# Two attentions with V as the stationary operand, in halves of TensorE's array; one group's z gemm computed during the second attention

## The chip, the cores and the metric

One core of one Trainium2 chip runs the whole program. The metric is device time in microseconds, from launch to end. TensorE (PE in the rows) multiplies, VectorE (DVE), ScalarE (ACT) and GpSimd (POOL) do the elementwise work, and SyncE (SP) issues most of the DMA transfers. In a matmul one operand is loaded into the array first (the stationary one) and the other is streamed through it (the moving one).

## The reference, cut to what matters

Two transformer-like blocks on 512 tokens of width 1024, everything in fp32. The first has a sliding-window attention and a memory attention (4 heads of 64 each), the second a top-k sparse attention with 16 heads on 4 key/value heads, a state-space branch (SSD) in 4 groups, and a mixture of experts. The parts that the change touches:

```python
# block 1, both attentions
p = softmax(logits)                                  # [head, query, key]
out = einsum('bhsm,bmhd->bshd', p, v)
# block 2
o = jnp.einsum('bqhgk,bqkhd->bqhgd', softmax(logits), v_sel)
...
y_ssd = ssd_chunked(xh, dt, A, B, C) + d_skip * xh
y_ssd = gated_group_rmsnorm(y_ssd, z, ssd_norm)      # silu(z) gates it; z = h @ W_z, in 4 groups of 512 columns
merged = sigmoid(gate_a) * (y_attn @ w_attn_branch) + sigmoid(gate_b) * (y_ssd @ w_ssd_branch)
```

## The kernel before

Tokens are worked on in 4 tiles of 128 (`NT = 4`, `P = 128`, `T = 512`). Almost all gemms are `gemm_t`: the weight is split into a rounded part `hi` (on ACT, line 173) and a rest `lo` (on DVE or POOL, line 175), and each product is three matmuls of 128 x 512 (lines 224 to 226). One unit of `gate` is 24 of these, and one 256-column unit pair of `w2` is 48.

The order is set by generators. `mix(main, filler)` runs a chain of dependent steps and after each pulls so much of a filler gemm as the step's number says; a scheduler then fixes the order on each engine. The engines run their queues in order.

The first block's attention (`pipeline` of `logits, expo, ptrans, pvmul, otrans` over 8 units, one per 128 queries and kind) has the gemms of u and z as filler. The second block's (32 units: key/value head `kv`, pair `c` of heads, query tile `b`) has the gate gemms as filler: `gates` is a chain of 16 units, the first 5 of which run ahead of it. In both, `pvmul` multiplies the transposed probabilities (`pT`, stationary, 128 x 128) by V (moving, 64 columns) (lines 755 and 1085), DVE scales the rows by the reciprocal `r` of the softmax sum while it takes the result out of PSUM, and `otrans` transposes the scaled tile on PE (lines 768 and 1098). In the second block the transposes of four query tiles fill one PSUM tile (`pacc`, of which there is one), which ACT copies out once per head pair.

After that `block2b` runs the SSD groups. `ssd_gemm(g)` gives five gemms of 48 matmuls for group g: b and c, xs in two halves, z in two halves. Those of b, c and xs end in `conv_silu` on DVE and ACT (lines 1184 to 1196), those of z in `silu_from` (lines 450 to 455). The gemms of group 0 run first; then `ssd_chain(0)` (chunks of 128 tokens: lines 1249 to 1302) runs with the gemms of group 1 as filler, and so on. The chain's product at line 1282 has its output in partitions 0 to 63 for one head and 64 to 127 for the next.

Of the kernel before, what the change touches and what calls it, by code (L numbers as in the profile page):

```python
# [19 lines left out]
P = 128  # L20
T = 512
# [22 lines left out]
class Ker:  # L44
# [412 lines left out]

    def pipeline(self, units, stages, need):
# [65 lines left out]
    def block1(self):  # L524
# [218 lines left out]
        def pvmul(u):  # L743
            kind, n = u
            wk, r, pT = st[u][1], *st[u][4:6]
            po = self.paux()
            nj = wk // P
            for h in range(4):
                for j in range(nj):
                    if kind == 0:  # L750
                        kt = n + 1 - nj + j
                        v = sv[:, kt * P + (h // 2) * 64:kt * P + (h // 2) * 64 + 64]
                    else:
                        v = mv[:, j * 256 + h * 64:j * 256 + h * 64 + 64]
                    nc.tensor.matmul(po[:, h * 64:h * 64 + 64], pT[j][:, h * P:(h + 1) * P], v,
                                     start=(j == 0), stop=(j == nj - 1))
            o = self.ms([P, 256], "ot")
            nc.vector.tensor_tensor(o.rearrange("p (h d) -> p h d", h=4),
                                    po[:, :256].rearrange("p (h d) -> p h d", h=4),
                                    r.unsqueeze(2).to_broadcast([P, 4, 64]), op=ALU.mult)  # L760
            st[u] = o

        def otrans(u):
            kind, n = u
            o = st.pop(u)
            po = self.paux()
            for c in range(2):
                nc.tensor.transpose(po[:, c * P:(c + 1) * P], o[:, c * P:(c + 1) * P], self.ident)
            nc.vector.tensor_copy(c2(oc if kind else ob)[:, :, n * P:(n + 1) * P],
                                  po[:, :256].rearrange("p (c t) -> p c t", c=2))  # L770
# [21 lines left out]
        mix(self.pipeline(units, (logits, expo, ptrans, pvmul, otrans), 4.5), f2)  # L792
# [77 lines left out]
    def block2(self, hh, hl, ssq):  # L870
# [181 lines left out]
        def expo(u):  # L1052
# [6 lines left out]
            r = self.sm([P, 2], "xr")  # L1059
            nc.vector.reciprocal(r, s)  # L1060
            st[u].append(r)
# [17 lines left out]
        def pvmul(u):  # L1079
            kv, c, b = u  # L1080
# [1187 lines left out]
```

## Time and profile before

| | us |
|---|---|
| median of three runs | 1304.72 |
| lowest, highest | 1301.74, 1309.18 |
| the profiled execution's own time | 1306.37 |
| its span, first to last instruction | 1304.7 |
| PE, DVE, ACT, POOL busy in the span | 1245.5, 882.0, 509.1, 429.5 |
| mean granted TensorE clock | 0.98 |

An engine counts as busy from the start of an instruction to its end. Matmuls overlap (the next starts before the one before has ended), so for PE the distance from start to start is what one costs, and PE may have room though it counts as busy. An fp32 matmul that isn't split stands in the trace as two records.

### The profile page before, as it was taken

How to read it: one execution, taken by the hardware profiler on the slowest of the kernel's cores; microseconds unless marked ns; L12 is line 12 of the kernel's file. 1: busy time of each engine (PE TensorE's matmuls, PEld its weight loads, DVE VectorE, ACT ScalarE, POOL GpSimd, SP SyncE). 2: the span in 40 equal slices, each digit the busy share in tenths (PEclk: the TensorE clock that was granted, in tenths of full speed). 3: DMA queues.
4: the chain of work that ended last, by engine and by line, in shares of the span. 5: the costliest groups of instructions: out<-in, count | busy, mean ns of one | idle time of the engine just before them, and what ended most of it. 6: DMA issues, size and time to landing. Idle time of an engine off the chain costs nothing. (4 is left out here: it accounts for less than half of the span.)

```text
span 1304.7 us, 18947 instructions
## 1 busy us (share of the span) xinstructions
PE 1245.5 (95%) x7045; PEld 975.2 (75%) x7045; DVE 882.0 (68%) x1700; ACT 509.1 (39%) x942; POOL 429.5 (33%) x474
## 2 busy tenths in 40 slices
PE   6899999999999999999999999999999999999787
PEld 5879888999987888888787887877889744544333
DVE  6598756658998676777988887888683532332255
ACT  6435553355543555443454442443333211111011
POOL 0373323169335431123463343436325110001020
PEclk8899999999999999999999999999999999999889
DMA  7234242052233221134334234385330999999992
GB/s 290 65 92 152 65 144 83 35 160 82 72 106 110 94 98 65 41 116 125 109 96 132 88 105 130 100 288 174 129 135 11 386 374 403 416 414 416 362 412 109
DMA packets 86911, 221.35 MB, mean 170 GB/s; under 512 B 8267, under 2 KB 31467, under 8 KB 86816
## 3 DMA queue, kind: packets, MB, share of 16 engines
q1 hardware_dynamic: 79808, 203.08, 44.6%
q10 hardware_dynamic: 4560, 10.26, 2.1%
q0 software_dynamic: 2448, 6.77, 1.4%
q8 instruction: 56, 0.92, 0.3%
q14 instruction: 39, 0.32, 0.1%
HBM read 205.97 MB, written 16.06 MB: 170 GB/s over the span
## 5 line engine op out<-in xcount | busy, mean ns | idle before, releaser
L175 POOL TENSOR_TENSOR wlo<-tb,whi 128x1024 fp32r<-128x1024 f32 x75 | 191.9, 2559 | 267.7 <-ACT whi L173 267.5
L224 PE MATMUL pmm<-tb,whi 128*128 128x512 f32 x600 | 238.7, 398 | 0.0
L226 PE MATMUL pmm<-tb,wlo 128*128 128x512 f32 x600 | 237.2, 396 | 0.0
L225 PE MATMUL pmm<-tb,whi 128*128 128x512 f32 x600 | 237.0, 395 | 0.0
L173 ACT CAST whi<-tb 128x1024 fp32r<-128x1024 f32 x139 | 144.8, 1044 | 138.6 <-PE pmm L225 57.0
L225 PEld LDWEIGHTS pmm<-tb,whi 128*128 128x128 f32 x600 | 114.0, 190 | 23.6 <-issue 0.9
L226 PEld LDWEIGHTS pmm<-tb,wlo 128*128 128x128 f32 x600 | 113.7, 189 | 24.0 <-issue 0.5
L224 PEld LDWEIGHTS pmm<-tb,whi 128*128 128x128 f32 x600 | 113.8, 190 | 23.2 <-issue 1.2
L175 DVE TENSOR_TENSOR wlo<-tb,whi 128x1024 fp32r<-128x1024 f32 x64 | 82.1, 1284 | 23.2 <-ACT whi L173 23.0
L225 PE MATMUL pmm<-t,whi 128*128 128x512 f32 (+1 forms) x208 | 79.4, 385 | 0.7 <-DVE t L356 0.7
L226 PE MATMUL pmm<-t,wlo 128*128 128x512 f32 (+1 forms) x208 | 79.4, 385 | 0.0
L224 PE MATMUL pmm<-t,whi 128*128 128x512 f32 (+1 forms) x208 | 79.4, 389 | 0.0
L1765 PE MATMUL pmm<-wr,xe 128*64 128x512 f32 x240 | 66.4, 596 | 0.0
L1772 DVE SCALAR_TENSOR_TENSOR th<-th,pmm 128x256 f32<-128x256 f32 x16 | 6.7, 420 | 86.0 <-ACT th L1771 86.0
L1771 ACT ACTIVATE th<-pmm,wcol 128x256 f32<-128x256 f32 x16 | 7.6, 474 | 136.9 <-PE pmm L1765 99.9
L1269 DVE TENSOR_SCALAR t<-t,acs 128x128 f32<-128x128 f32 x128 | 43.8, 408 | 24.2 <-DMA t<-scr_a 24.2
L1190 DVE SCALAR_TENSOR_TENSOR t<-cv,cwh,t 128x512 f32<-128x512 f32 x72 | 56.6, 840 | 0.3 <-ACT t L1187 0.3
L334 PE MATMUL pmm<-whi,tb 128*128 128x256 f32 x192 | 54.8, 285 | 0.0
L336 PE MATMUL pmm<-whi,tb 128*128 128x256 f32 x192 | 54.6, 284 | 0.0
L335 PE MATMUL pmm<-wlo,tb 128*128 128x256 f32 x192 | 54.4, 283 | 0.0
L1057 ACT ACTIVATE tL<-tL,xm 128x128 f32<-128x128 f32 (+3 forms) x64 | 35.4, 554 | 30.6 <-DVE xm L1049 30.4
L225 PEld LDWEIGHTS pmm<-t,whi 128*128 128x128 f32 x208 | 39.2, 188 | 8.4 <-DVE t L356 1.1
(452 smaller groups left out, 2960.3 us busy)
## 6 DMA issues: line engine op xcount, KB each, us to landing
wr<-in_we_dram SPq DMA_DIRECT2D x89, 512.0 KB, 10.1
tb<-in_w_dram SPq DMA_DIRECT2D x78, 512.0 KB, 3.6
tb<-in_we_dram SPq DMA_DIRECT2D x53, 512.0 KB, 10.1
rx<-in_we_dram SPq DMA_DIRECT2D x50, 512.0 KB, 9.0
tb<-in_wo_dram SPq DMA_DIRECT2D x16, 512.0 KB, 3.7
tb<-in_wg_dram SPq DMA_DIRECT2D x16, 512.0 KB, 3.6
t<-scr_a SPq DMA_DIRECT2D x16, 512.0 KB, 5.8
tb<-in_wsb_dram SPq DMA_DIRECT2D x16, 512.0 KB, 3.7
```

The lines of the kernel that those rows point to most:

```text
L173: nc.vector.tensor_copy(hi, raw) if dve_hi else nc.scalar.copy(hi, raw)
L175: f = lambda: (nc.gpsimd if pool_lo else nc.vector).tensor_tensor(lo, raw, hi, op=ALU.subtract)
L224: nc.tensor.matmul(ps[c][:, :n], hi[:, s], xh[k], start=first, stop=False)
L225: nc.tensor.matmul(ps[c][:, :n], hi[:, s], xl[k], start=False, stop=False)
L226: nc.tensor.matmul(ps[c][:, :n], lo[:, s], xh[k], start=False, stop=last)
L334: nc.tensor.matmul(o, xh[k][:, ts], hi[:, s], start=(k == 0 and t % 2 == 0), stop=False, **kw)
L335: nc.tensor.matmul(o, xh[k][:, ts], lo[:, s], start=False, stop=False, **kw)
L336: nc.tensor.matmul(o, xl[k][:, ts], hi[:, s], start=False, stop=(k == 7), **kw)
L1057: nc.scalar.activation(L3[:, j], L3[:, j], AF.Exp, bias=m[:, j:j + 1], scale=0.125, accum_out=s[:, j:j + 1])
L1190: nc.vector.scalar_tensor_tensor(y, x[:, i:T + i], w(ct, i), y, op0=ALU.mult, op1=ALU.add)
L1269: nc.vector.tensor_scalar(h8(ab)[:, h], h8(ab)[:, h], self.acs[:, c, 8 * g + h:8 * g + h + 1], 0.0, op0=ALU.subtract, op1=ALU.min)
L1765: nc.tensor.matmul(pg[h * 64:h * 64 + 64], xe[d][:, e + h], w[:, j * 512:(j + 1) * 512], start=(d == 0), stop=(d == 7))
```

## The change

It has two parts. In both attentions V becomes the stationary operand (128 x 64) and the transposed probabilities the moving one (128 columns). Two heads write to partitions 0 to 63 and 64 to 127 of one PSUM tile, so that the result is already transposed and `otrans` is gone. As the queries are now in the columns, the reciprocals must be in the columns too: the new `rcp_t` multiplies a column of `r`, broadcast to 64 columns (stationary), by the identity matrix (moving). ACT copies that to SBUF, and DVE multiplies the two, in the second block once per head pair for four query tiles.

The other part: the z columns of SSD group 0 become four more units of `gates` (16 to 19), are scaled, and written to DRAM. In `block2b` the two z gemms of group 0 are gone; `z_load` reads the four tiles, ACT does the tanh and DVE the last product. The other groups are as before.

```diff
--- before
+++ after
@@ -454,6 +454,11 @@
+
+    def rcp_t(self, out, r):
+
+        for j in range(2):
+            self.nc.tensor.matmul(out[j * 64:j * 64 + 64], r[:, j:j + 1].to_broadcast([P, 64]), self.ident, start=True, stop=True, skip_group_check=True)
@@ -741,33 +746,31 @@  (block1)
         def pvmul(u):
...
-            for h in range(4):
+            for c in range(2):
                 for j in range(nj):
-                    if kind == 0:
...
-                    nc.tensor.matmul(po[:, h * 64:h * 64 + 64], pT[j][:, h * P:(h + 1) * P], v,
-                                     start=(j == 0), stop=(j == nj - 1))
-            o = self.ms([P, 256], "ot")
-            nc.vector.tensor_tensor(o.rearrange("p (h d) -> p h d", h=4),
-                                    po[:, :256].rearrange("p (h d) -> p h d", h=4),
-                                    r.unsqueeze(2).to_broadcast([P, 4, 64]), op=ALU.mult)
-            st[u] = o
-
-        def otrans(u):
...
+                    for i in range(2):
+                        h = 2 * c + i
...
+                        nc.tensor.matmul(po[i * 64:i * 64 + 64, c * P:(c + 1) * P], v, pT[j][:, h * P:(h + 1) * P],
+                                         start=(j == 0), stop=(j == nj - 1), skip_group_check=True)
+            pr = self.paux()
             for c in range(2):
-                nc.tensor.transpose(po[:, c * P:(c + 1) * P], o[:, c * P:(c + 1) * P], self.ident)
-            nc.vector.tensor_copy(c2(oc if kind else ob)[:, :, n * P:(n + 1) * P],
-                                  po[:, :256].rearrange("p (c t) -> p c t", c=2))
+                self.rcp_t(pr[:, c * P:(c + 1) * P], r[:, 2 * c:2 * c + 2])
+            rt = self.ms([P, 256], "ot")
+            nc.scalar.copy(rt, pr[:, :256])
+            nc.vector.tensor_tensor(c2(oc if kind else ob)[:, :, n * P:(n + 1) * P],
+                                    po[:, :256].rearrange("p (c t) -> p c t", c=2),
+                                    rt.rearrange("p (c t) -> p c t", c=2), op=ALU.mult)
@@ -901,17 +904,18 @@  (block2)
-        self.gd = tc.dram_tile([16, P, T], F32, name="scr_g")
+        self.gd = tc.dram_tile([20, P, T], F32, name="scr_g")
...
                 nc.vector.tensor_tensor(t_, ps[0], rbh, op=ALU.mult)
-                nc.scalar.activation(t_, t_, AF.Tanh)
+                if i < 16:
+                    nc.scalar.activation(t_, t_, AF.Tanh)
                 nc.scalar.dma_start(self.gd[i], t_)
             return self.gemm_t([("wg", i)], hh, hl, [list(range(8))], f, cols=1)
-        gates = chain(*[gate(i) for i in range(16)])
+        gates = chain(*[gate(i) for i in range(20)])
@@ -1077,28 +1081,23 @@  (block2)
-            for j in range(2):
-                for t, pT, i in pts:
-                    nc.tensor.matmul(po[:, j * 64:j * 64 + 64], pT[:, i * 256 + j * P:i * 256 + (j + 1) * P],
-                                     v4[:, t, kv * 64:kv * 64 + 64], start=(t == 0), stop=(t == b))
-            o = self.ms([P, P], "ot")
...
-        def otrans(u):
             kv, c, b = u
             if b == 0:
                 st["o"] = self.pacc()
             po = st["o"]
-            nc.tensor.transpose(po[:, b * P:(b + 1) * P], st.pop(u), self.ident)
+            for t, pT, i in st.pop(u)[2]:
+                for j in range(2):
+                    nc.tensor.matmul(po[j * 64:j * 64 + 64, b * P:(b + 1) * P], v4[:, t, kv * 64:kv * 64 + 64],
+                                     pT[:, i * 256 + j * P:i * 256 + (j + 1) * P], start=(t == 0), stop=(t == b), skip_group_check=True)
             if b == NT - 1:
-                o = self.t2()
-                nc.scalar.copy(o, po)
+                pr = self.paux()
+                r = st.pop(("r", kv, c))
+                for t in range(NT):
+                    self.rcp_t(pr[:, t * P:(t + 1) * P], r[:, t])
+                rt, o = self.t2(), self.t2()
+                nc.scalar.copy(rt, pr)
+                nc.vector.tensor_tensor(o, po, rt, op=ALU.mult)
                 nc.gpsimd.dma_start(self.yad[2 * kv + c], o)
@@ -1220,7 +1219,21 @@  (ssd_gemm)
+        def z_load():
+            ths = []
+            for k, z in enumerate(d["z"]):
+                nc.sync.dma_start(z, self.gd[16 + k])
+            for z in d["z"]:
+                th = self.t2()
+                nc.scalar.activation(th, z, AF.Tanh)
+                ths.append(th)
+            yield 0
+            for z, th in zip(d["z"], ths):
+                nc.vector.scalar_tensor_tensor(z, th, 1.0, z, op0=ALU.add, op1=ALU.mult)
+        first = [self.gemm_t(u2(0), hh, hl, KK, bc_done)] + [self.gemm_t(u2(1 + i), hh, hl, KK, xs_done(i)) for i in range(2)]
+        if g == 0:
+            return first + [z_load()]
@@ -2111,10 +2124,11 @@  (host)
-    A["wg"] = units(np.concatenate([ga, gb], axis=1), 8, P)
+    A["wg"] = units(np.concatenate([ga, gb, z2[:, :512]], axis=1), 8, P)
```

On PE inside the second attention (`paux`, `pacc`: PSUM; `t_503`: V; `pT`: probabilities; `pmm`: a gate), before, one unit near its middle:

```order
L1098 MATMUL pacc_4926<-cst,ot_4933 128x128
L224 MATMUL pmm_5093<-tb_1959,whi_4692 128x512
L225 MATMUL pmm_5093<-tb_1959,whi_4692 128x512
L226 MATMUL pmm_5093<-tb_1959,wlo_4694 128x512
L224 MATMUL pmm_5093<-tb_1960,whi_4692 128x512
L225 MATMUL pmm_5093<-tb_1960,whi_4692 128x512
L226 MATMUL pmm_5093<-tb_1960,wlo_4694 128x512
L1085 MATMUL paux_4994<-t_503_2769,pT_4940 128x64 x2
L1085 MATMUL paux_4994<-t_503_2769,pT_4945 128x64
L1085 MATMUL paux_4994<-t_503_2769,pT_4940 128x64 x2
L1085 MATMUL paux_4994<-t_503_2769,pT_4945 128x64
L1072 MATMUL paux_5003<-cst,tL_4875 128x128 x4
```

The transpose (L1098), a piece of gate and the product V by probabilities (L1085) take turns. The change, in the same place of another head pair:

```order
L224 MATMUL pmm_5088<-tb_1976,whi_4690 128x512
L225 MATMUL pmm_5088<-tb_1976,whi_4690 128x512
L429 MATMUL paux_5019<-cst,t_506_2788 128x128 x4
L1091 MATMUL pacc_4857<-pT_4994,t_503_2785 64x128 x4
L1091 MATMUL pacc_4857<-pT_5001,t_503_2785 64x128 x4
L461 MATMUL paux_5054<-cst,xr_4731 64x128 x8
L1076 MATMUL paux_5068<-cst,tL_4942 128x128 x2
L1049 MATMUL paux_5079<-t_668_3755,t_818_4534 128x384
```

The transposes are gone, the product stands in 64 x 128 form, and at a head pair's last tile the eight matmuls of the reciprocals (L461) stand behind it. In all the program has 160 products and 64 of L461 in 39 such stretches, with 128 x 128 work ahead and behind each; in the first attention 60 and 32 in 10 stretches.

On PE at the end of the gates in the second attention, before:

```order
L226 MATMUL pmm_5480<-tb_1959,wlo_5096 128x512
L224 MATMUL pmm_5480<-tb_1960,whi_5094 128x512
L1098 MATMUL pacc_5160<-cst,ot_5224 128x128
L225 MATMUL pmm_5480<-tb_1960,whi_5094 128x512
L226 MATMUL pmm_5480<-tb_1960,wlo_5096 128x512
L1085 MATMUL paux_5291<-t_503_2769,pT_5231 128x64 x2
L1072 MATMUL paux_5302<-cst,tL_5186 128x128 x2
L1085 MATMUL paux_5291<-t_503_2769,pT_5238 128x64 x2
L1085 MATMUL paux_5291<-t_503_2769,pT_5231 128x64 x2
```

After the last of these gate matmuls 86 of the 160 products (L1085) follow without filler. With the change the last gate matmul stands here:

```order
L1049 MATMUL paux_5819<-t_678_3836,t_1042_5451 128x512
L1050 MATMUL paux_5819<-t_679_3837,t_1042_5451 128x512
L225 MATMUL pmm_5870<-tb_1976,whi_5579 128x512
L226 MATMUL pmm_5870<-tb_1976,wlo_5581 128x512
L1091 MATMUL pacc_5799<-pT_5807,t_503_2785 64x128 x4
L1076 MATMUL paux_5843<-cst,tL_5769 128x128
L1076 MATMUL paux_5850<-cst,tL_5769 128x128
L1049 MATMUL paux_5861<-t_678_3836,t_1058_5514 128x128
```

There 38 of the 160 products are left behind it.

On DVE in SSD group 0 (`mm`: the z tiles; L175: a weight's rest; L1190, L1196 and in the change L1189, L1195: the convolution), before, between the convolution of the second xs half and the chain's first chunk:

```order
L1190 SCALAR_TENSOR_TENSOR t_1266_6209<-cv_6298,cwh,t_1266_6209 128x512
L450 TENSOR_TENSOR mm_5997<-pmm_6317,tb_2610 128x512
L1196 SCALAR_TENSOR_TENSOR t_1266_6209<-t_1282_6309,t_1266_6209 128x512
L450 TENSOR_TENSOR mm_5998<-pmm_6318,tb_2610 128x512
L1196 SCALAR_TENSOR_TENSOR t_1266_6209<-t_1283_6311,t_1266_6209 128x512
L175 TENSOR_TENSOR wlo_6391<-tb_6323,whi_6389 128x1024
L455 SCALAR_TENSOR_TENSOR mm_5997<-t_1292_6381,mm_5997 128x512
L455 SCALAR_TENSOR_TENSOR mm_5998<-t_1293_6382,mm_5998 128x512
L450 TENSOR_TENSOR mm_5999<-pmm_6387,tb_2610 128x512
L450 TENSOR_TENSOR mm_6000<-pmm_6388,tb_2610 128x512
L1257 TENSOR_TENSOR cb_6469<-paux_6464,cst 128x128
L1255 TENSOR_TENSOR t_1307_6467<-paux_6459,dt 128x512
```

The change:

```order
L1189 SCALAR_TENSOR_TENSOR t_1214_6297<-cv_6386,cwh,t_1214_6297 128x512
L1195 SCALAR_TENSOR_TENSOR t_1214_6297<-t_1230_6397,t_1214_6297 128x512
L1270 TENSOR_TENSOR cb_6433<-paux_6428,cst 128x128
L1183 TENSOR_TENSOR cv_6534<-pmm_6439,tb_2626 128x512
L1195 SCALAR_TENSOR_TENSOR t_1214_6297<-t_1231_6399,t_1214_6297 128x512
L1287 TENSOR_TENSOR t_1236_6421<-t_1236_6421,cb_6433 128x1024
L1232 SCALAR_TENSOR_TENSOR mm_6085<-t_1232_6409,mm_6085 128x512
L1183 TENSOR_TENSOR cv_6537<-pmm_6440,tb_2626 128x512
L1232 SCALAR_TENSOR_TENSOR mm_6086<-t_1233_6411,mm_6086 128x512
L1232 SCALAR_TENSOR_TENSOR mm_6087<-t_1234_6413,mm_6087 128x512
L1232 SCALAR_TENSOR_TENSOR mm_6088<-t_1235_6415,mm_6088 128x512
L175 TENSOR_TENSOR wlo_6604<-tb_6445,whi_6602 128x1024
```

The four products with PSUM (L450) are gone from here, the last products (L455, now L1232) are left, and the convolution of group 1 (L1183) begins among them.

## Rows read from the trace of the kernel before

**Rows 1.** The page, first part: busy time of each engine.

```profile
PE 1245.5 (95%) x7045; PEld 975.2 (75%) x7045; DVE 882.0 (68%) x1700; ACT 509.1 (39%) x942; POOL 429.5 (33%) x474
```

**Rows 2.** Busy time by stage; columns as in the first line.

```profile
core 0: us, PE busy (x) PEld busy (x) DVE busy (x) ACT busy (x) POOL busy (x), PEclk, DMA share, GB/s
105.00:215.00 110.00, 109.56 (x648) 95.58 (x647) 73.56 (x124) 55.80 (x130) 29.55 (x16) 1.00 0.31 101
393.30:541.90 148.60, 143.73 (x930) 126.69 (x928) 109.30 (x359) 78.77 (x200) 46.78 (x74) 0.99 0.26 82
542.10:677.70 135.60, 132.39 (x650) 107.52 (x649) 113.54 (x184) 58.71 (x82) 51.49 (x39) 0.99 0.36 108
584.80:670.00 85.20, 82.16 (x416) 65.70 (x414) 75.61 (x112) 38.13 (x55) 38.20 (x26) 0.98 0.39 113
```

**Rows 3.** Busy time, second attention, from its last gate matmul on.

```profile
497.40:541.90 44.50, 41.97 (x334) 38.06 (x332) 34.40 (x125) 26.23 (x75) 2.24 (x4) 1.00 0.14 49
```

**Rows 4.** Timeline of PE inside the second attention: start, length, instructions.

```profile
423.79 0.39 PE L224 MATMUL pmm<-tb,whi 128*128 128x512 f32 x1
424.02 0.60 PE L429 MATMUL paux<-cst,t 128*128 128x128 f32 x4
424.46 0.27 PE L1098 MATMUL pacc<-cst,ot 128*128 128x128 f32 x1
424.57 1.45 PE L1085 MATMUL paux<-t,pT 128*128 128x64 f32 x12
425.85 1.05 PE L1072 MATMUL paux<-cst,tL 128*128 128x128 f32 x8
```

**Rows 5.** Timeline of PE around one SSD product in array halves (L1282).

```profile
642.57 0.39 PE L224 MATMUL pmm<-tb,whi 128*128 128x512 f32 x1
642.88 1.09 PE L1282 MATMUL pacc<-t,t 128*64 128x128 f32 x16
643.91 0.50 PE L225 MATMUL pmm<-tb,whi 128*128 128x512 f32 x1
644.25 0.40 PE L226 MATMUL pmm<-tb,wlo 128*128 128x512 f32 x1
```

**Rows 6.** Timeline of PE, first and last of 80 gemm matmuls in a row.

```profile
542.19 0.40 PE L225 MATMUL pmm<-tb,whi 128*128 128x512 f32 x1
...
560.15 0.40 PE L226 MATMUL pmm<-tb,wlo 128*128 128x512 f32 x1
```

**Rows 7.** Group of the product in the second attention.

```profile
L1085 PE MATMUL paux<-t,pT 128*128 128x64 f32 x320 | 40.6, 272 | 1.8 <-DVE pT L1075 1.4
```

**Rows 8.** Groups of PE in its last 44.5 us.

```profile
L1085 PE MATMUL paux<-t,pT 128*128 128x64 f32 x172 | 22.1, 273 | 1.8 <-DVE pT L1075 1.4
L1072 PE MATMUL paux<-cst,tL 128*128 128x128 f32 x80 | 12.3, 276 | 0.3 <-ACT tL L1057 0.3
L1045 PE MATMUL paux<-t,t 128*128 128x384 f32 (+3 forms) x28 | 10.6, 382 | 0.0
...
L1098 PE MATMUL pacc<-cst,ot 128*128 128x128 f32 x17 | 4.8, 284 | 0.3 <-DVE ot L1088 0.3
```

**Rows 9.** Groups of DVE in 584.8 to 670.0 us.

```profile
L1196 DVE SCALAR_TENSOR_TENSOR t<-t,t 128x512 f32<-128x512 f32 x9 | 13.5, 1527 | 0.2 <-ACT t L1193 0.2
L175 DVE TENSOR_TENSOR wlo<-tb,whi 128x1024 fp32r<-128x1024 f32 x6 | 8.0, 1328 | 0.7 <-ACT whi L173 0.7
...
L450 DVE TENSOR_TENSOR mm<-pmm,tb 128x512 f32<-128x512 f32 x6 | 4.0, 681 | 1.9 <-PE pmm L226 1.9
```

**Rows 10.** Timeline of DVE: the same two instructions, alone and beside GpSimd.

```profile
583.61 1.28 DVE L1196 SCALAR_TENSOR_TENSOR t<-t,t 128x512 f32<-128x512 f32 x2
...
642.34 4.35 DVE L1196 SCALAR_TENSOR_TENSOR t<-t,t 128x512 f32<-128x512 f32 x2 [0.15 <-ACT t L1193]
```

**Rows 11.** Timeline of POOL beside the second of these.

```profile
643.30 2.84 POOL L175 TENSOR_TENSOR wlo<-tb,whi 128x1024 fp32r<-128x1024 f32 x1
```

**Rows 12.** Timeline of PE: end of the chain of group 0.

```profile
670.17 1.02 PE L369 MATMUL paux<-ones,t 128*128 128x1 f32 x8 [1.25 <-DVE t L393]
```

More of the change, by code (lines that the diff above doesn't have):

```diff
@@ L747, in pvmul @@
             nj = wk // P
[L748 removed]
+            for c in range(2):
                 for j in range(nj):
[L750 to L770 removed]
+                    for i in range(2):
+                        h = 2 * c + i
+                        if kind == 0:
+                            kt = n + 1 - nj + j
+                            v = sv[:, kt * P + c * 64:kt * P + c * 64 + 64]
+                        else:
+                            v = mv[:, j * 256 + h * 64:j * 256 + h * 64 + 64]
+                        nc.tensor.matmul(po[i * 64:i * 64 + 64, c * P:(c + 1) * P], v, pT[j][:, h * P:(h + 1) * P],
+                                         start=(j == 0), stop=(j == nj - 1), skip_group_check=True)
+            pr = self.paux()
+            for c in range(2):
+                self.rcp_t(pr[:, c * P:(c + 1) * P], r[:, 2 * c:2 * c + 2])
[4 more added lines that the diff above has]
+                                    rt.rearrange("p (c t) -> p c t", c=2), op=ALU.mult)
+            st.pop(u)
             done.add(u)
@@ L791, in block1 @@
         f2 = chain(self.gemm_t(u1(6), hh, hl, KK, u_done(1)), z[0], z[1], z[2])
-        mix(self.pipeline(units, (logits, expo, ptrans, pvmul, otrans), 4.5), f2)
+        mix(self.pipeline(units, (logits, expo, ptrans, pvmul), 4.5), f2)
         run(f2)
@@ L1058, in expo @@
                                      accum_out=s[:, j:j + 1])
-            r = self.sm([P, 2], "xr")
-            nc.vector.reciprocal(r, s)
-            st[u].append(r)
+            if u[2] == 0:
+                st["r", u[0], u[1]] = self.sm([P, NT, 2], "xr")
+            nc.vector.reciprocal(st["r", u[0], u[1]][:, u[2]], s)
         def ptrans(u):
@@ L1112, in attn @@
         def attn():
-            for i, _ in enumerate(self.pipeline(units, (logits, expo, ptrans, pvmul, otrans), 0)):
+            for i, _ in enumerate(self.pipeline(units, (logits, expo, ptrans, pvmul), 0)):
                 if i % 8 in (1, 2, 3, 4, 5, 6):
@@ L1200, in ssd_gemm @@
         nc = self.nc
-        u2 = lambda i: [("w2", 2 * (8 + 5 * g + i)), ("w2", 2 * (8 + 5 * g + i) + 1)]
+        u2 = lambda i: [("w2", 2 * (8 + max(5 * g - 2, 0) + i) + j) for j in range(2)]
         d = self.grp[g] = {}
@@ L1222, in z_done @@
             return f
-        return ([self.gemm_t(u2(0), hh, hl, KK, bc_done)] + [self.gemm_t(u2(1 + i), hh, hl, KK, xs_done(i)) for i in range(2)]
+        def z_load():
[12 more added lines that the diff above has]
+            return first + [z_load()]
+        return (first
                 + [self.gemm_t(u2(3 + i), hh, hl, KK, z_done(i)) for i in range(2)])
@@ L2113, in host @@
     for g in range(4):
-        cols += [bs[:, g * P:(g + 1) * P], cs[:, g * P:(g + 1) * P], xs[:, g * 512:(g + 1) * 512],
-                 z2[:, g * 512:(g + 1) * 512]]
+        cols += [bs[:, g * P:(g + 1) * P], cs[:, g * P:(g + 1) * P], xs[:, g * 512:(g + 1) * 512]]
+        if g:
+            cols.append(z2[:, g * 512:(g + 1) * 512])
     A["w2"] = units(np.concatenate(cols, axis=1))
-    A["wg"] = units(np.concatenate([ga, gb], axis=1), 8, P)
+    A["wg"] = units(np.concatenate([ga, gb, z2[:, :512]], axis=1), 8, P)
     A["wab"] = units(f("w_attn_branch_2")[0])
```

7 lines of the change are left out of this document (removed).

## The prediction

> **What bounds the kernel now.** I read the page's busy times first: PE is busy for 95% of the span, DVE for 68% [rows 1]. That is an average over stages, so the next view was busy time by stage, for the three that the change touches [rows 2]. In the first attention (105 to 215 us) PE is busy 109.6 of 110.0 us. In the second (393.3 to 541.9) it is 143.7 of 148.6, with DVE at 109.3. In SSD group 0 (542.1 to 677.7) it is 132.4 of 135.6, but from 584.8 to 670.0, where the chain of the group runs beside the gemms of group 1, DVE is busy 75.6 of 85.2 us: nearly a second bound. So the first two stages are priced by what a matmul costs PE, and the third by PE and DVE both.
>
> As a busy PE can still have room, I took the cost of a matmul from distances between starts in the timeline. A gemm matmul of 512 columns: 79 steps from 542.19 to 560.15, 0.227 us each [rows 6]. The old product V by probabilities: 12 records in 1.28 us (424.57 to 425.85), 0.107 each, and a lone transpose in front 0.11 (424.46 to 424.57) [rows 4]. The new form isn't in the attentions, but SSD has it: L1282, 128 x 64 stationary, 128 columns, two halves in turn. 16 records last 1.09 us [rows 5]. Less the last one's own latency (0.27, as for the lone transpose in rows 4), that is 0.82 over 15 steps: 0.055 each, though it streams twice the columns.
>
> The same rows show what going in and out of this form costs. From the gemm matmul at 642.57 to the one at 644.25 there are 1.68 us; two gemm steps are 0.45, 16 records 0.88, and 0.35 is left over [rows 5]. With 128 x 128 work in place of it there is next to none: L429 begins one step (0.23) after the gemm's last start, and L1098, L1085 and L1072 follow in step [rows 4].
>
> **The change part by part.** *First attention.* Gone: 60 products, two records each, at 0.107, 12.8 us, and 16 transposes at 0.11, 1.8. New: 60 products and 32 reciprocal matmuls, 184 records at 0.055, 10.1, and 10 stretches in the new form at 0.3, 3.0. Sum -1.5 us. I take 0.3 for a stretch: 0.35 is the gemm row's, and where the next work is fp32 too, less is left over (from 643.91 to 644.25 the gemm behind takes 0.34, 0.11 more than its step). With 0 it would be -4.5, with 0.45 (short stretches in which the halves don't pair up) 0.
>
> The Trainium skill says the same against this change ("TensorEngine Tiling (Array Packing)", Tiling Modes, Key Properties): a change of tiling mode, not of tile, drains TensorE. It gives no price. Rows 5 agree, and only the 0.35 us from them is used. The same page (Performance Considerations) advises just this swap with column tiling where the moving side has at most 64 columns, for up to 2x; by that rule alone, without the drains, the sum below would be 12 us lower, which is part of the first rival.
>
> *Second attention.* Gates: 4 more units of 24 matmuls, 96 x 0.227 = +21.8. Products: 320 records [rows 7] from 0.107 to 0.055, -16.6. Transposes: 32 x 0.11 = -3.5. Reciprocals: 64 matmuls, 128 records at 0.055, +7.0. Stretches: 39, of which some nine lie in the part without filler, where PE has slack: 30 x 0.3 = +9.0 (0 to 17). Filler: in the last 44.5 us there is none now; own work there is 172 x 0.107 + (80 + 17) x 0.11 + 9 or so for 56 matmuls of the logits (28 at L1045 and as many behind it, 0.11 to 0.23 each by width) + 1 for transposes of q = 39, so about 5 us of slack lie there, more than the 2.5 that PE is shown idle [rows 3, 8]. With the change only 38 of 160 products stand behind the last gate, so I count 3.6 of the 5 as used (1 to 5). Sum +14.1 us.
>
> DVE loses 32 scalings and gains 8 of 512 columns and 4 for z (0.68 each as L450 [rows 9]); it has 39 us of room in this stage [rows 2]. The z tiles go to DRAM by ACT's queue, four transfers of 256 KB under 100 us of attention. A wait is new: the single `pacc` is held from the first product of a head pair to DVE's multiplication, and the next pair's first product, with all of PE behind it, waits for the chain reciprocals, ACT copy, DVE. That is some 3 us; a step of the pipeline is 148.6 / 36 = 4.1 us, so it is covered while there is filler. Without cover it costs 1 to 2 us at each of the last two pairs, which is in what I left of the slack.
>
> *SSD group 0.* PE loses 96 gemm matmuls, -21.8, if nothing else holds it. But of DVE's 75.6 us only four L450 (0.68 each) and two weight splits (1.33 each) go [rows 9], 5.4 us. The last products stay, now on z read back. So DVE still has 70.2 us, and from 584.8 on the stage can't be shorter than that and what DVE idles. Its idle time is 9.6 us now [rows 2]. Part of it is a wait for gemms that will no longer be late, so I leave 1.5: 71.7 in place of 85.2, -13.5. Bounds: -21.8 if PE alone decides, -5.4 if DVE idles as now. At the end PE waits for DVE even now: L369 needs the sum of squares and sat idle 1.25 us before it [rows 12]. DVE's times here hold delays by GpSimd: two L1196 take 1.28 us alone and 4.35 where a POOL split runs from 643.30 to 646.14 [rows 10, 11]; L1196's mean is 1.53 in this stretch [rows 9]. GpSimd's work stays nearly the same in less time, so I don't expect this to shrink.
>
> z_load is queued on SP behind weight loads and ahead of the chain's first loads; z is needed only after the chain, so a late load costs nothing by itself. But the four L1232 stand ahead of the first chunk's next steps on DVE, so a load that is late by microseconds would stop these.
>
> **The sum.** -1.5 + 14.1 - 13.5 = -0.9 us on the profiled execution's own 1306.4 (the span of 1304.7 and 1.7 around it), so 1305.5. That execution is 1.7 above the median, so against the median of 1304.7 the forecast is 1304. The mixture of experts and the later groups stand in the same order as before and move with it.
>
> **The rivals.** *Faster.* The drains hide behind waits (-9.0 in the second attention, -3.0 in the first), and PE rather than DVE decides SSD group 0 (-8.3 more). All of it is -21.2, so 1283.5; either half gives about 1292 to 1296. For it speaks that DVE's order begins group 1's convolution earlier, so that some of its idle time goes; against it the drain in rows 5 and 75.6 of 85.2.
>
> *Slower.* DVE gives back only the 5.4 us that it loses in work, since in a stage with less gemm time every wait for a scalar, a load or GpSimd comes out on PE. That is +8.1, so 1312. It decides from about 8 us of idle time on DVE from 584.8 to the end of the chain. For it speak the stalls by GpSimd; against it that the chain's loads come earlier relative to their use.
>
> *The halves do not run side by side.* Then a record costs 0.107, as for 128 x 128: 632 records (184 and 448) more by 0.052, +33, so 1337. Rows 5 speak against it, the shapes being the same; but in some stretches one product of a pair stands alone.
>
> **How the numbers follow.** A run's spread is about 0.3%, so 0.5% (6.5 us) is what this kernel's measurement can tell from no change. Chances: the near-cancelling sum 0.44, the faster rival 0.32, the slower 0.20, the halves not side by side 0.04. The likeliest case alone spans 1298 to 1311. For 8 in 10 the range goes to 1290, which leaves out the far end of the faster rival, and to 1313, which takes in the slower one. Faster by over 0.5% 0.33, within 0.44, slower 0.23.
>
> **What would show it.** In the profile after, the product of the second attention should be some 18 us busy in place of 40.6, and the distance over a stretch about 0.3 us more than its records; the second attention about 163 us long; no long part without gates at its end. From the end of the attention to the start of group 1's chain about 122 us, with DVE above 93% busy from the first convolution on, and PE idle several times by 1 to 3 us for DVE. I am wrong if the granted clock falls in that stage (PE's idle time then costs twice), if PE waits for `pacc` in the middle of the attention, or if the drains don't show.

## The result, and the profile after

The changed kernel is slower: 1314.34 us (median of 15 runs, 1311.36 to 1321.66) against 1307.06 for the kernel before (15 runs beside them, 1301.74 to 1314.42); ratio 1.0057, 95% interval 1.0041 to 1.0074. The forecast was 1304 us, no change, with a range up to 1313. It stood on 1304.72 us, the median of the first three runs of the kernel before; fifteen runs put that kernel at 1307.06. So 2.3 of the 10.3 us between forecast and result lie in this base, and the change itself is worth +7.3 us where -0.9 was forecast.

The page, first part, busy time of each engine; [rows 1] is the line of before:

```profile
PE 1245.6 (95%) x7189; PEld 954.0 (73%) x7189; DVE 883.2 (67%) x1668; ACT 512.2 (39%) x950; POOL 422.3 (32%) x474
```

PE's busy time is the same to 0.1 us, over a span that is 8.9 us longer (1313.6 against 1304.7). So over the whole span it is PE's idle time that has grown; the stages themselves change by far more, in opposite directions. Busy time by stage, columns as in [rows 2]: the second attention, SSD group 0 (from the attention's end to the first transposes of group 1's chain), and the part of it in which the group's chain runs beside the gemms of group 1:

```profile
394.60:561.50 166.90, 163.13 (x1121) 128.52 (x1119) 113.41 (x338) 83.89 (x205) 51.15 (x76) 0.99 0.30 92
561.50:686.80 125.30, 115.10 (x562) 92.27 (x560) 111.13 (x180) 54.91 (x78) 42.60 (x37) 0.96 0.38 110
604.00:676.80 72.80, 62.62 (x327) 48.60 (x325) 72.40 (x107) 34.48 (x52) 29.48 (x24) 0.96 0.38 105
```

Against [rows 2] the attention is 18.4 us longer (148.6 to 167.0, from the first logits to the first gemm matmul behind the last product) and group 0 is 10.6 shorter (135.9 to 125.3). DVE is busy 72.40 of 72.80 us beside the chain: it has next to no idle time left there. PE's granted clock has gone from 0.99 to 0.96 in group 0.

The costliest groups of the new form in the second attention, which answer to [rows 7]:

```profile
L1091 PE MATMUL pacc<-pT,t 128*64 128x128 f32 x320 | 26.6, 283 | 0.0
L461 PE MATMUL paux<-cst,xr 128*64 128x128 f32 x128 | 9.7, 277 | 0.0
```

The products went from 40.6 to 26.6 us busy, not to 18, and PE never waits for `pacc` in this stage. What makes up the difference is seen in the timeline of PE around one stretch of products in the second attention:

```profile
454.56 0.39 PE L226 MATMUL pmm<-tb,wlo 128*128 128x512 f32 x1
454.79 0.39 PE L224 MATMUL pmm<-tb,whi 128*128 128x512 f32 x1
455.11 0.44 PE L1091 MATMUL pacc<-pT,t 128*64 128x128 f32 x4
455.48 0.50 PE L225 MATMUL pmm<-tb,whi 128*128 128x512 f32 x1
455.81 0.39 PE L226 MATMUL pmm<-tb,wlo 128*128 128x512 f32 x1
```

From 454.79 to 455.81 there are 1.02 us; two gemm steps (0.45) and four records at 0.055 (0.22) leave 0.35 for going in and out, as in [rows 5]. Four records gain 4 x 0.052 = 0.21 us on the old form, so a stretch this short loses 0.14.

PE's waits in group 0 of the changed kernel (total, times, longest):

```profile
PE paux L369 <- DVE t L393: 5.5, 1, 5.5
PE pacc L1295 <- DVE t L1297: 1.4, 1, 1.4
PE pacc L1295 <- DVE t L1268: 1.3, 1, 1.3
PE paux L1300 <- DVE t L1314: 1.0, 1, 1.0
```

With two below a microsecond they are 10.2 us, against 2.0 and 1.2 before. The first is L369 of [rows 12], which idled 1.25 us then. Timeline of PE around it, and the clock by windows behind it:

```profile
670.97 0.39 PE L226 MATMUL pmm<-tb,wlo 128*128 128x512 f32 x1
676.82 1.87 PE L369 MATMUL paux<-ones,t 128*128 128x1 f32 x8 [5.46 <-DVE t L393]
678.54 0.77 PE L224 MATMUL pmm<-tb,whi 128*128 128x512 f32 x1
679.12 0.63 PE L225 MATMUL pmm<-tb,whi 128*128 128x512 f32 x1
679.54 0.63 PE L226 MATMUL pmm<-tb,wlo 128*128 128x512 f32 x1
```

```profile
670.00:677.00 7.00, 1.54 (x7) 0.96 (x7) 6.64 (x11) 6.79 (x12) 0.10 (x1) 0.86 0.26 76
677.00:682.00 5.00, 5.00 (x16) 4.30 (x17) 5.00 (x7) 3.01 (x5) 3.91 (x2) 0.51 0.09 15
682.00:687.00 5.00, 5.00 (x28) 4.28 (x27) 0.75 (x2) 1.05 (x1) 0.63 (x2) 1.00 0.54 195
```

PE idles 5.46 us, and then is granted 0.51, the lower level (1.2 GHz), for 5 us: a gemm step takes 0.42 us (679.12 to 679.54) in place of 0.227. Half the clock for 5 us is, as an estimate, another 2.5 us.

So of z's 21.8 us, 7 went into new waits (10.2 less 3.2, nearly all of it for DVE) and 2.5 into the clock, which leaves 12.3; 10.6 came back, and the last 1.7 I can't place. What comes after group 0 is the same within a microsecond.

### The profile page after: what moved, and what is told of

Read it like the earlier page. It is cut to its first block, busy times and chain, and to the rows that moved or that the text cites. A ratio compares the mean times of both kernels' runs of the same rounds, so it can differ in the third digit from the quotient of the medians.

```text
span 1313.6 us, 19205 instructions
## 1 busy us (share of the span) xinstructions
PE 1245.6 (95%) x7189; PEld 954.0 (73%) x7189; DVE 883.2 (67%) x1668; ACT 512.2 (39%) x950; POOL 422.3 (32%) x474
## 5 line engine op out<-in xcount | busy, mean ns | idle before, releaser
L175 POOL TENSOR_TENSOR wlo<-tb,whi 128x1024 fp32r<-128x1024 f32 x75 | 190.0, 2533 | 317.0 <-ACT whi L173 301.9
L175 DVE TENSOR_TENSOR wlo<-tb,whi 128x1024 fp32r<-128x1024 f32 x64 | 85.0, 1330 | 31.4 <-ACT whi L173 31.2
L1189 DVE SCALAR_TENSOR_TENSOR t<-cv,cwh,t 128x512 f32<-128x512 f32 x72 | 62.4, 919 | 0.3 <-ACT t L1186 0.3
L1282 DVE TENSOR_SCALAR t<-t,acs 128x128 f32<-128x128 f32 x128 | 46.9, 434 | 19.5 <-DMA t<-scr_a 19.5
```

Of the source, the lines that this page charges most:

```text
L175: f = lambda: (nc.gpsimd if pool_lo else nc.vector).tensor_tensor(lo, raw, hi, op=ALU.subtract)
L1189: nc.vector.scalar_tensor_tensor(y, x[:, i:T + i], w(ct, i), y, op0=ALU.mult, op1=ALU.add)
L1282: nc.vector.tensor_scalar(h8(ab)[:, h], h8(ab)[:, h], self.acs[:, c, 8 * g + h:8 * g + h + 1], 0.0, op0=ALU.subtract, op1=ALU.min)
```

## The experiments

Below, "attention" is the second one as above, and "to the merge" runs from its end to the first instruction of DVE that merges the branches (all four SSD groups lie in it; the order of instructions at a group's border changes from kernel to kernel, so a shorter stretch compares badly). First and last start of that merge before, and after:

```profile
L1398 DVE TENSOR_TENSOR mB<-mB,mm x8: 678/682/685, 953.2 to 972.6; 128x512 f32<-128x512 f32 x8
```

```profile
L1411 DVE TENSOR_TENSOR mB<-mB,mm x8: 679/682/687, 963.0 to 982.4; 128x512 f32<-128x512 f32 x8
```

Times are medians; ratios stand against the kernel before, run beside each (its medians were 1305.5 to 1307.4). The two stretches come from one profiled execution each. The attention repeats within 1.2 us where the order of its products is the same (166.9 to 167.3 seven times); to the merge, kernels that keep z in place show 410.5 to 417.9. The two highest of these, e1 and e11, come from executions 6.9 and 3.4 us above their kernel's median.

| kernel | time us | ratio, 95% interval | attention | to the merge |
|---|---|---|---|---|
| before | 1307.1 | | 148.6 | 411.3 |
| after | 1314.3 | 1.0057 (1.0041 to 1.0074) | 167.0 | 401.4 |
| e1_halves_only | 1309.1 | 1.0020 (0.9998 to 1.0043) | 150.3 | 417.9 |
| e2_z_only | 1318.1 | 1.0081 (1.0050 to 1.0112) | 168.6 | 400.6 |
| e3_one_stretch | 1307.8 | 1.0016 (0.9997 to 1.0036) | 161.3 | 400.9 |
| e4_more_changes | 1321.8 | 1.0120 (1.0082 to 1.0157) | 176.3 | 398.9 |
| e5_silu_early | 1312.2 | 1.0037 (1.0013 to 1.0061) | 167.3 | 397.3 |
| e6_decay_act | 1316.4 | 1.0074 (1.0046 to 1.0101) | 167.0 | 402.0 |
| e7_one_stretch_no_z | 1300.6 | 0.9952 (0.9926 to 0.9979) | 142.4 | 413.3 |
| e8_both | 1310.2 | 1.0025 (0.9999 to 1.0051) | 160.2 | 401.8 |
| e9_buffers_only | 1314.6 | 1.0039 (1.0018 to 1.0060) | 166.9 | 399.5 |
| e10_fewer_taps | 1316.7 | 1.0064 (1.0040 to 1.0088) | 167.0 | 406.6 |
| e11_fewer_taps_no_z | 1308.5 | 0.9998 (0.9976 to 1.0020) | 149.1 | 417.8 |
| e12_one_stretch_silu | 1308.6 | 0.9993 (0.9970 to 1.0015) | 161.3 | 399.5 |
| e13_three_buffers | 1313.3 | 1.0054 (1.0035 to 1.0073) | 167.0 | 401.0 |
| e14_three_buffers_taps | 1304.9 | 1.0005 (0.9986 to 1.0024) | 167.0 | 394.1 |
| e15_one_stretch_no_z_three | 1297.9 | 0.9933 (0.9909 to 0.9957) | 142.3 | 410.5 |
| e16_z_at_its_best | 1304.3 | 0.9976 (0.9956 to 0.9995) | 161.3 | 400.2 |

### Which half of the change loses

**e1_halves_only** is the changed kernel with the diff's lines on z taken back.

> The halves and the direct transposition in both attentions as in the changed kernel; z of the first SSD group stays where it was (16 gates, z from w2). Theory: 41 stretches of the half form in the second attention and 10 in the first take about 0.35 us each (17.9 us in all), nearly what the shorter products and the missing transposes give back (16.6 + 3.5 in the second, 4.5 in the first, less 7.0 and 3.1 for the reciprocals), and the rest of the loss is z's. Then this kernel is 0 to 4 us below the kernel before (1303 to 1307 us), with the second attention 145 to 149 us long (148.6 before). Rival A, the halves alone carry the loss: 1312 to 1316 us, attention 155 us or longer. Rival B, the halves gain what their records say and z alone loses it: 1297 us or less, attention under 140 us.

**e2_z_only** is the kernel before with those lines alone (20 gates, z_load, the layout of the weights).

> The kernel before with z of the first SSD group as four more gates, kept in DRAM and loaded back; products and transposes as before. Theory: the attention grows by 16 to 22 us (96 passes of 0.227 us less what fits into the idle time of its tail) and the stretch from its end to the first chain of the second SSD group shrinks from 135.9 to about 125 us, since VectorE and not TensorE sets its length there; sum +5 to +10 us, 1312 to 1317 us. Rival A (z costs nothing net, the halves lose): 1305 to 1309 us. Rival C (the tail of the attention has room for z): below 1302 us.

Measured: the halves alone +2.5 us, not told from zero (the interval ends at 0.9998), with the attention at 150.3 us in place of 148.6; z alone +11.4 us, with 20.1 us more in the attention and 10.7 less to the merge. z loses, and the halves give next to nothing: rivals A and B of e1 both fall, and so do A and C of e2. Both kernels are slower than their theories said: e1 lies 2 us above its 1303 to 1307 (its attention 1.3 above 149), e2 1 us above its 1312 to 1317. The two don't add up to the change: with z in the attention the halves make it 1.6 us shorter (168.6 to 167.0), without z they make it longer.

### What a change of form costs

**e3_one_stretch**: products wait for the fourth query tile of their head pair, so that they come together.

```
-            if b == 0:
-                st["o"] = self.pacc()
-            po = st["o"]
-            for t, pT, i in st.pop(u)[2]:
...
+            if b < NT - 1:
+                return
+            po = self.pacc()
+            for b in range(NT):
+                for t, pT, i in st.pop((kv, c, b))[2]:
...
-        t = (self.pq or self.px).tile(..., bufs=4 if tag in ("pT", "ot") else 2)
+        t = (self.pq or self.px).tile(..., bufs=8 if tag == "pT" else 4 if tag == "ot" else 2)
```

> The changed kernel with the products of all four query tiles of a head pair issued together behind the last one's transposes (8 buffers for the transposed probabilities instead of 4). The half form then comes in 16 stretches instead of 39 in the second attention; records and work are the same. Theory (each change of form costs about 0.35 us): second attention 8 us shorter than the changed kernel's 166.9, so about 159 us, time about 1306 us. Rival A (the half form is slow by its own records, or VectorE and ScalarE set the pace of the attention): no change, 1313 to 1316 us. Rival D (the later products hold up the chain of the head pairs): slower, above 1317 us.

Timeline of PE in e3_one_stretch, one stretch (L1092 is the product there):

```profile
445.34 0.40 PE L226 MATMUL pmm<-tb,wlo 128*128 128x512 f32 x1
445.67 1.09 PE L1092 MATMUL pacc<-pT,t 128*64 128x128 f32 x16
446.69 0.45 PE L1049 MATMUL paux<-t,t 128*128 128x384 f32 x1
```

Sixteen records take 1.02 us from start to start, so the half form runs as fast as in [rows 5] once it is left alone. The attention is 5.7 us shorter for 23 stretches fewer, 0.25 us each; the time fell by 6.6 us. Both stay 2 us above the expectation (159 and 1306), and rivals A and D are out.

**e4_more_changes** does the opposite. Its added transposes start a new accumulation in the bank of the running sums, so those sums lack their first key tiles; only its time is used.

```
             for t, pT, i in st.pop(u)[2]:
+                if t and b < NT - 1:
+                    nc.tensor.transpose(po[:, 3 * P:4 * P], pT[:, :P], self.ident)
```

> The changed kernel with 24 more transposes of 128x128 between half-form products in the second attention, written into a part of the accumulator that later products overwrite: 58 stretches of the half form instead of 39. Theory: 24 transposes of 0.11 us and 19 more changes of form of 0.35 us, +9.3 us: second attention 176 us, time 1323 to 1325 us. Rival A (a change of form costs nothing, the loss has another place): +2.6 us, 1316 to 1318 us.

The attention is 176.27 us, +9.3 to the tenth: 24 x 0.11 = 2.6 us for the transposes and (9.3 - 2.6) / 19 = 0.35 us for each added stretch. Rival A is out. The time is at 1321.8 rather than 1323 to 1325; the stretch to the merge was 2.5 us shorter in that execution.

**e9_buffers_only** is e3's second edit without the first.

> The changed kernel with 8 buffers for the transposed probabilities and nothing else, the control for e3_one_stretch and e7_one_stretch_no_z; 39 stretches of the half form in the second attention as in the changed kernel. Theory: the number of changes of form made e3_one_stretch faster, so nothing moves here: attention 167 us, 1313 to 1316 us. Rival G (waits for a buffer were what e3_one_stretch took away): attention about 161 us, 1307 to 1309 us.

The attention is 166.9 us: the buffers did nothing, the order did it all. Rival G is out.

**e7_one_stretch_no_z** is e1_halves_only with e3's edits.

> The halves without the move of z (as in e1_halves_only), the products of a head pair issued together: 25 stretches of the half form in the second attention instead of 41. By the 0.25 us per stretch that e3_one_stretch gave back (5.7 us for 23) the attention is 4 us shorter than that of e1_halves_only (150.3), about 146 us, and the time 1304 to 1306 us, at or just below the kernel before. Rival F (without z the last 45 us of the attention are set by ScalarE and VectorE, not by TensorE): the 10 stretches taken out of the first part count, the rest not: 148 us, 1307 us.

1300.6 us, faster than both kernels; the attention is 142.4 us, 6.7 to 7.9 below the 149.1 and 150.3 that e11 and e1 show with the same code for it. By e3's 0.25 us the 16 stretches taken out are worth 4.0 of that, and I have no experiment for the rest; the time is 3 us below what was expected. The traces show where it lies: up to the last gate matmul e7 has 9 stretches where e11 has 24 and takes 2.4 us less (106.6 and 108.9), and behind it, with 16 stretches and 17, 4.4 us less (35.8 and 40.1). Work has moved ahead of that matmul, and PE idles 3.3 us behind it in place of 4.6. Rival F is out by its figure (148 us), but the last part gains by this, not by fewer stretches.

### Why z's passes come back by half

**e5_silu_early**: ACT's tanh and DVE's product for z go with the gates.

```
+                else:
+                    th = self.t2()
+                    nc.scalar.activation(th, t_, AF.Tanh)
+                    nc.vector.scalar_tensor_tensor(t_, th, 1.0, t_, op0=ALU.add, op1=ALU.mult)
... (and the same two steps taken out of z_load)
```

> The changed kernel with the silu of z finished in the attention (tanh and the product there, z itself is stored): four products of 1.22 us each (4.7 us in all) leave VectorE's work in the first SSD group. Theory: VectorE sets the length of that stretch (72.4 us busy of 72.8 between 604 and 676.8 us), so it falls from 125.3 to about 121 us, and the time to about 1310 us; VectorE has room in the attention. Rival E (TensorE, the weights or the queue of SyncE set the stretch): 125 us as before, 1313 to 1316 us.

To the merge 4.1 us less (group 0 by itself 121.5 us), near the 4.7 of DVE; 1312.2 us, 2 below the changed kernel, and above the 1310 expected. The intervals of the two kernels overlap, so the times alone don't show this gain.

**e6_decay_act** gives ScalarE the decays of group 0.

```
+                if g == 0:
+                    nc.scalar.activation(h8(ab)[:, h], h8(ab)[:, h], AF.Relu,
+                                         bias=self.acs[:, c, 8 * g + h:8 * g + h + 1], scale=-1.0)
... (other groups as before; the Exp behind it takes scale=-1.0 in group 0)
```

> The changed kernel with the differences of the decays of the first SSD group (32 instructions of VectorE, 0.46 us each, 14.8 us) done by ScalarE as Relu with a bias per partition, its Exp then with the sign turned. Theory: VectorE sets the first SSD group, TensorE's 115.1 us are next; the stretch falls from 125.3 to 115 to 118 us and the time to 1304 to 1307 us. Rival E (VectorE is busy there but does not set the length): 124 to 126 us, no change, 1313 to 1316 us; if ScalarE, in order with the casts of the weights, takes over: 120 us or more.

A miss: 125.2 us for group 0, 402.0 to the merge, where rival E had it. Waits of ACT and DVE in e6's group 0:

```profile
ACT t L1283 <- DMA t<-scr_a: 8.1, 4, 4.2
DVE t L1189 <- ACT t L1186: 6.8, 3, 6.0
```

ACT waits for the loads of the decays (`scr_a`), and in its order the first step of the convolution (L1186) stands behind them, for which DVE waits. This run took DVE's work away and put an ACT wait in its place, so it says nothing on whether DVE's work sets the length. **e8_both** is e3, e5 and e6 together, and has the same fault.

> z moved, halves in one stretch for a head pair (e3_one_stretch), the silu of z finished in the attention and the decays of the first SSD group on ScalarE. Theory: the attention stays at 161 us, the first SSD group goes to TensorE's bound of about 115 us instead of 125.6: 1296 to 1299 us, faster than both kernels. Rival E (VectorE does not set that stretch): 1307 us as e3_one_stretch.

A miss by 11 us: it came to 1310.2 us, above e3 alone, with 129.5 us for group 0 and PE waiting 7.9 us for DVE at the end of the chain.

**e10_fewer_taps** therefore leaves work out instead, and **e11_fewer_taps_no_z** does so with z in place.

```
-            for i in range(3):
+            for i in range(2 if ct in (0, 1, 2, 3, 16, 20) else 0, 3):
```

> The changed kernel without two of the convolution's taps on the six tiles of the first SSD group: 12 instructions of VectorE of 0.91 us (10.9 us) are left out, nothing is put elsewhere. Theory: VectorE sets the first SSD group once z has gone; the stretch falls from 125.3 us to TensorE's 115 to 117 us, the time to 1304 to 1307 us. Rival E (VectorE is busy but another wait sets the length, as e6_decay_act, with 125.2 us, may mean): 123 to 126 us, 1312 to 1316 us.

> The halves without the move of z (e1_halves_only) with the same two taps of the first SSD group left out. Theory: with z's 96 passes in it that stretch is set by TensorE (134.2 us busy of 137.3), so it stays at 134 to 137 us, 1306 to 1309 us, and what z's move gives back when VectorE is out of the way is this stretch less that of e10_fewer_taps: 18 to 21 us, nearly all of the 21.8 us of its passes. Rival E: the stretch shortens here as well, to 130 us or less.

e10 shows no gain at all (1316.7 us; group 0 125.9 us, rival E's figure; 406.6 to the merge). My theory that DVE's work alone sets the stretch falls here. DVE's longest wait in e10's group 0:

```profile
DVE t L1282 <- DMA t<-scr_a: 9.6, 3, 4.1
```

DVE now waits 9.6 us for the decays (1.5 in the changed kernel): 10.9 us of work were replaced by a wait. The decays have two buffers, and SP's load for a later chunk waits until an earlier one's product has read its buffer. SP's wait in e10 for that product (L1253 issues the load; the changed kernel has no such wait):

```profile
SPq L1253 <- PE pacc L1295: 6.5, 2, 5.1
```

In e11 nothing moves against e1 (417.8 and 417.9 to the merge; group 0 137.7 and 137.3), as expected where PE is idle for only 3 to 4 us of group 0. But e11's group 0 less e10's is 11.8 us, not the 18 to 21 expected.

**e13_three_buffers** and **e14_three_buffers_taps** give the decays a third buffer, without and with the taps left out.

```
-            k.nt2, k.nt4 = 14, 2
+            k.nt2, k.nt4 = 14, 3
```

> The changed kernel with three buffers instead of two for the decays of the SSD chunks, nothing else. Theory (VectorE first, the loads second): VectorE is busy 99.5% between 604 and 676.8 us, so an earlier load does not help: the first SSD group stays at 124 to 126 us, the time at 1312 to 1316 us. Rival J (the loads alone set it): 118 us or less, 1307 us or less.

> e10_fewer_taps (two taps of the convolution left out in the first SSD group, 10.9 us of VectorE) with three buffers for the decays. Theory (VectorE first, the loads behind it): with both out of the way the stretch falls to 115 to 119 us, the time to 1306 to 1309 us. Rival K (neither: TensorE waits for the steps of the group's chain through VectorE, ScalarE and GpSimd, whatever the two do, since z's passes no longer stand between them): 123 us or more, 1313 us or more.

The buffer alone does nothing (401.0 to the merge, 1313.3 us; rival J is out), the taps alone nothing (406.6), both together 7.3 us (394.1; 1304.9 us against 1314.3). DVE's wait for the decays in e14, and PE's longest in its group 0:

```profile
DVE t L1282 <- DMA t<-scr_a: 3.0, 1, 3.0
PE paux L369 <- DVE t L393: 2.7, 1, 2.7
```

That looks like two limits one behind the other, DVE's work and the loads of its decays. But group 0 up to its own border is 132.0 us in e13 and 122.8 in e14, above what was expected of both, and the traces put most of e14's gain elsewhere. The third buffer serves all four groups. A border that doesn't move is the sum of squares at the end of a group's chain (L369): in the kernels that move z the same gemm matmuls lie ahead of it for groups 1 to 3. For these groups, in the changed kernel and then in e14:

```profile
754.80 1.05 PE L369 MATMUL paux<-ones,t 128*128 128x1 f32 x8 [0.16 <-DVE t L393]
848.28 1.05 PE L369 MATMUL paux<-ones,t 128*128 128x1 f32 x8 [0.54 <-DVE t L393]
926.58 0.95 PE L369 MATMUL paux<-ones,t 128*128 128x1 f32 x8
```

```profile
749.70 1.05 PE L369 MATMUL paux<-ones,t 128*128 128x1 f32 x8
842.80 1.05 PE L369 MATMUL paux<-ones,t 128*128 128x1 f32 x8
917.60 0.95 PE L369 MATMUL paux<-ones,t 128*128 128x1 f32 x8
```

From the attention's end (561.54 and 558.82) to the first of these are 193.3 and 190.9 us, so groups 0 and 1 together gain 2.4. Group 2 gains 0.4 and group 3, which neither z nor the taps touch, 3.5 (78.3 to 74.8). Group 3 takes 74.8 us in all four kernels with the third buffer, and 76.8 to 82.2 in every other. Up to the end of group 1 e10 takes 195.2 us and e13 197.9.

So with both out of the way z's move gives back 14.6 us by the end of group 1 (against before, 205.5) or 16.4 (against e11, 207.3), where the changed kernel has 12.2; the full 21.8 is not shown. Rival K stays open: its 123 us for group 0 are missed by 0.2, its time by a gain that lies mostly in later groups, and PE still idles 8.1 us in e14's group 0 (10.2 in the changed kernel). Each edit also moves the order of the other engines a little, so these runs price the pair, not each wait in it.

**e12_one_stretch_silu** (e3 and e5), **e15_one_stretch_no_z_three** (e7 with the third buffer) and **e16_z_at_its_best** (e12 with it) look for the best kernel.

> The best form of the change as a whole: z moved, its silu finished in the attention (e5_silu_early), the products of a head pair in one stretch (e3_one_stretch). Theory: attention 161 us, first SSD group 121.5 us, 1303 to 1306 us: at the kernel before, and some 3 us above e7_one_stretch_no_z, in which z stays. Rival H (the two gains are one and the same): 1307 to 1310 us.

> e7_one_stretch_no_z (z stays, products of a head pair in one stretch, 1300.6 us) with three buffers for the decays. In the first SSD group TensorE is busy 131.0 of 133.2 us there, so nothing is to be had in it; in the later groups the traces show waits for the decays of a few us at most: 1297 to 1302 us, at most 3 us below e7_one_stretch_no_z.

> e12_one_stretch_silu (z moved, its silu finished in the attention, products of a head pair in one stretch) with three buffers for the decays. It differs from e15_one_stretch_no_z_three (1297.9 us) by z alone. Theory: the attention stays at 161.3 us, 19 us above e15_one_stretch_no_z_three; of VectorE's work only 4.7 us have left the first SSD group, so the stretch from the attention to the merge comes to 394 to 398 us, 13 to 17 us below the 410.5 of e15: 1301 to 1305 us, so moving z still loses 3 to 7 us. Rival L (with three buffers the passes come back in full): 1294 to 1299 us.

e12 is at 1308.6 us, above its 1303 to 1306, and no better than e3 alone (rival H); e5's gain didn't add in the time. e15 is the best kernel measured, 1297.9 us, 0.67% below before; what the third buffer adds to e7 (2.7 us) lies within the two intervals. e16 differs from it by z alone and is 6.4 us slower: the attention pays 18.9 us, and to the merge only 10.3 come back (rival L is out). Its 1304.3 us lie in the expectation, its 400.2 to the merge don't (394 to 398). Up to the end of group 1 it takes 196.5 us and e12 192.8: with all taps in place the third buffer made this part longer in each pair (e13 by 4.6, e15 against e7 by 4.3), and why is open.

## Why the prediction was wrong, point by point

**First attention** (-1.5). Right in size: from its first logits to the next block's start it fell by 1.1 us (109.6 to 108.5). Work ahead of it, which the change doesn't touch, took 2.3 us more in this execution, which is why the second attention begins 1.2 us later.

**Second attention** (+14.1, measured +18.4). Two terms failed, and together they are the 4.3 us. "Filler ... I count 3.6 of the 5 as used": z alone made the attention 20.1 us longer (e2), so its 21.8 us found 1.7 us of room. "Stretches ... 30 x 0.3 = +9.0", with nine assumed free: records, transposes and reciprocals make -16.6 - 3.5 + 7.0 = -13.1, and measured is -1.6 for the halves beside z, so the 39 stretches cost 11.5 us. That is 0.3 for every one, or 33 at e4's 0.35, so whether a few were free stays open; seven, not nine, lay behind the last gate matmul. The mechanism and its price were right (0.25 to 0.35 by e3 and e4); the number that pay it was too low, and so was what was left of the filler's slack. The wait for `pacc`, put at some 3 us without a row, never showed on PE here.

The Trainium skill ("TensorEngine Tiling (Array Packing)", Tiling Modes, Key Properties) says that a change of mode drains TensorE. e3 and e4 agree, at 0.25 and 0.35 us for each stretch. The same page of the Trainium skill (Performance Considerations) advises the swap with 2x column tiling where the moving side has 64 columns. In the records the factor showed, 0.107 to 0.055 us; in 41 stretches, 26 of them of 2 to 8 records, going in and out took nearly all of it (e1), in 25 longer ones it did not (e7).

**SSD group 0** (-13.5, measured -10.6; to the merge -9.9). The stretch that the sum priced came out near: from the same step of the convolution to the last step of the sum of squares on DVE, 85.2 us (584.8 to 670.0) became 72.2, where 71.7 was forecast.

```profile
604.56:676.76 72.20, 62.06 (x324) 48.12 (x323) 71.80 (x106) 33.88 (x51) 29.48 (x24) 0.96 0.38 105
```

Its two terms were off and cancel, which is luck: DVE kept 71.8 us of work, not 70.2, and idled 0.4, not 1.5. The step that failed is that the account ended there, with nothing for what follows. From PE's L369 to group 1's chain 7.6 us became 10.0 (670.17 to 677.73 before, 676.82 to 686.80 after), because PE's clock had fallen in its wait, and that is 2.4 of the 2.9 us missed. The wait itself grew from 1.25 to 5.46 us; it comes with z's move (1.2 us in e1, 3.3 in e2). My list named the falling clock as what would make me wrong; it had no price in the sum. What I had no idea of either, the two buffers of the decays, cost nothing by itself in the changed kernel (e13).

**The rivals.** The slower one, with a chance of 0.20, had nearly the right end (1312), but by luck: it wants some 8 us of idle time on DVE beside the chain, and DVE idled 0.4 us there; the stretch shrank by 13.0 us and not by 5.4. The loss came from the attention (4.3 us) and from the clock behind the chain. The faster rival is out: the drains are paid (e4), and PE did not decide group 0; even with taps left out and a third buffer it idles 8.1 us in it (e14). Halves side by side: shown by e3's 16 records in 1.02 us.

**What would show it.** Products at 26.6 us in place of 18: with short stretches the drain is inside the busy time (22.0 in e3). DVE above 93%: 92% from the first convolution to the end of the chain (96.8 of 104.7 us), 99.5% from 604.0 on. PE idle several times by 1 to 3 us for DVE: three times, and once by 5.5. PE waited for `pacc` nowhere in the attention.

## What to carry to other kernels

Work moved out of a stage takes its cover with it: before moving matmuls, look at what would wait if they weren't there, one limit behind the other (here DVE's work, the double-buffered loads behind it, and the clock after the wait at the chain's end), and expect back only the distance to the next of them. A form that halves a matmul's time but has a fixed price for going in and out pays only in long stretches, so group the work first; leaving z where it was and grouping the products made a gain of 0.48% out of the same change (e7), with a third buffer 0.67% (e15). When two parts of a change aim at different stages, run each alone, and place a gain in the trace before giving it a cause: nearly half of e14's lies in a group that its taps don't touch.

## What was not expected of the hardware

A change between the full array and column halves costs about 0.35 us in and out for fp32 records (e4: 19 stretches, 6.7 us; 0.25 by e3), as long as six records of the half form.

A single wait of PE of 5.46 us was followed by 5 us at a granted clock of 0.51, which is 2.5 us, an estimate, on top of the wait. But its length alone doesn't tell: before, the clock stayed at 1.00 behind 1.25 us of idle time at the same place [rows 12], while in e1 it fell behind 1.22. The clock by windows before, then the wait and the clock in e1:

```profile
671.10:676.80 5.70, 5.70 (x26) 4.74 (x27) 4.33 (x7) 2.29 (x4) 4.39 (x2) 1.00 0.36 97
```

```profile
671.99 1.02 PE L369 MATMUL paux<-ones,t 128*128 128x1 f32 x8 [1.22 <-DVE t L393]
```

```profile
674.00:676.50 2.50, 2.50 (x7) 1.93 (x7) 1.97 (x3) 2.05 (x3) 2.50 (x2) 0.50 0.00 0
```

e5, e10 and e14, which cut this wait to 2.1 to 2.7 us, were still granted 0.50 behind it.
